# Attention block of a hybrid decoder: last block's transposes, last pair's outputs and two value banks are moved

## The chip, the cores and the metric

One Trainium2 chip, one of its cores. The time is that of one launch on the device in microseconds, the median of several runs. The engines are named as in the profile: PE is TensorE's matmul and PEld its weight load, DVE is VectorE, ACT is ScalarE, POOL is GpSimd, SP is SyncE. They run asynchronously and wait for each other on semaphores. Matmul results land in PSUM banks, from which ACT and DVE read them.

## What is computed

Two pre-norm residual layers over a sequence of 512 tokens with 1024 channels: an S5 state-space layer, then a forgetting attention, each followed by a gated convolutional FFN. The change lies in the attention:

```python
def fox_mixer(h, w_in, b_f, w_out):
    """logit[t,s] = q_t.k_s/sqrt(d) + sum_{s<j<=t} log f_j, causal."""
    proj = h @ w_in
    q = proj[..., :D_MODEL].reshape(Bsz, S, FOX_HEADS, FOX_HEAD_DIM) * (FOX_HEAD_DIM ** -0.5)
    k = proj[..., D_MODEL:2 * D_MODEL].reshape(Bsz, S, FOX_HEADS, FOX_HEAD_DIM)
    v = proj[..., 2 * D_MODEL:3 * D_MODEL].reshape(Bsz, S, FOX_HEADS, FOX_HEAD_DIM)
    f_logit = proj[..., 3 * D_MODEL:]
    log_f = jax.nn.log_sigmoid((f_logit + b_f).astype(f32))
    F = lax.cumsum(log_f, axis=1).transpose(0, 2, 1)
    ...
        s = jnp.einsum('bhqd,bshd->bhqs', q_blk, k).astype(f32)
        s = s + Fq[..., None] - F[:, :, None, :]
        s = jnp.where(causal, s, -jnp.inf)
        p = jax.nn.softmax(s, axis=-1)
        return jnp.einsum('bhqs,bshd->bqhd', p.astype(v.dtype), v)
    ...
    return o @ w_out
```

There are 16 heads of 64 channels, that is 8 pairs of heads, and 4 blocks of 128 queries. All is float32 at the surface.

## The kernel before

Every large product is done in three matmuls: each operand is split into a high part (a rounded copy, made on ACT) and a low part (the rest, made on DVE), and high x high, high x low and low x high are accumulated in one PSUM bank. `put_parts` (L236 and L237) does such a split: one ACT copy, then one DVE subtraction. Weights arrive by DMA as `raw`, are split into `w_hi` and `w_lo`, and are used at L253 (`mms`).

PSUM has eight banks, in two pools of four: `mm` (tile name `mmp`) and `aux`. A new tile of a pool takes the pool's banks in turn and has to wait until the last reader of its bank is done. The program's text is not always the order of issue: the framework arranges the instructions of each engine when the kernel is built, by when it takes their operands to be ready, and on the chip each engine then goes through its own list in order.

The attention runs as follows.

- `fox_values` (L1104) computes the values and the forget gates' logits. `values` (L1125) takes a set of value quarters `q` and token blocks `b`, holds one bank for each (q, b), and loops over the 8 contraction tiles; then it splits each result into `v` and, for quarter 0, adds the bias to the logits (`ft`, L1143). Group 1 is quarters 0 and 1 on blocks 0 and 1, group 2 the same quarters on blocks 2 and 3, groups 3 and 4 are quarters 2 and 3 on all blocks. During group 1 the norm of the second half of the tokens is still being applied on ACT and DVE (L386 to L390). Behind group 2 the log of the forget gates is computed in many small DVE instructions.
- The query and key projections (L1190) are 16 tiles `m` with 8 contraction tiles each. After each contraction tile (three matmuls, one step) `unit` is called, which counts steps and issues whatever is due at that step.
- When the key tile of pair `hp` is done, `attend` (L1199) enters that pair's work into the list of due steps, by `ORDER` (L48), relative to the step count at that moment: `s0` computes the pair's scores (L1229), the masked minimum on DVE (L1241), the exponential on ACT (L1245), the normalization on POOL (L1250); `t0` to `t3` transpose query block 0 to 3 of the probabilities (L1259) and split them from an aux bank into `phi` and `plo`; `o0` and `o1` (`weigh`, L1267) multiply by the values of the pair's first and second head (L1276), copy and add the result into `ot` (L1282, L1283), and after `o1` split it into `v`'s place as the operand of the output product. So the work of a pair lies between the projections of the next one.
- t0 and t1 take one aux bank each, t2 and t3 two each (one for each head), o0 and o1 one each, the scores four (six for the last pair).
- The output product (`fox`, L1153) does the first four output tiles together (`head=4`): one contraction tile is 12 matmuls, and then `unit(3)` is called, which goes through three steps at once. The work of the last pair therefore lies between the contraction tiles of this head; its own result is the last of the eight contraction tiles, tile 7.

Of the kernel before, what the change touches and what calls it, by code (L numbers as in the profile page):

```python
# [8 lines left out]
F32 = mybir.dt.float32  # L9
# [8 lines left out]
P = 128  # L18
D = 1024
KT = D // P  # L20
S = 512
# [23 lines left out]
QK = 6  # L45


ORDER = ((3, "s0"), (8, "t0"), (8, "t1"), (10, "t2"), (12, "t3"), (17, "o0"), (18, "o1"))  # L48


class Trunk:
# [1019 lines left out]
class Kernel(S5):  # L1071
# [32 lines left out]
    def fox_values(self, pool, x):  # L1104

        nc = self.nc

        self.v = pool.tile([P, KT, NB, 2, 2, HD], F32R, name="v")
        ft = pool.tile([P, NB, NH], F32, name="ft")
        bf = self.fox_bf  # L1110
        W = VH * HD
        xhi, xlo = x

        def load(q):

            src = self.io["fox_v"][q - 1] if q else self.io["fox_vf"]
            n, step = (W, 4) if q else (W + NH, 3)
            out = []
            for a in range(0, KT, step):
                j = min(step, KT - a)  # L1120
                hi, lo = self.split(src[:, a:a + j, :], [P, j, n])
                out += [(hi[:, i, :], lo[:, i, :]) for i in range(j)]
            return out

        def values(qs, blocks, w):  # L1125
            todo = [(q, b) for q in qs for b in blocks]
            ps = {k: self.mm.tile([P, S], F32, name="mmp") for k in todo}
            for k in range(KT):
                for q, b in todo:
                    hi, lo = w[q][k]  # L1130
                    n = W if q else W + NH
                    tb = slice(b * P, (b + 1) * P)
                    for i, (xt, wt) in enumerate(((xhi, hi), (xhi, lo), (xlo, hi))):
                        self.last_mm = nc.tensor.matmul(  # L1134
                            ps[q, b][:, :n], xt[:, k, tb], wt, start=(k == 0 and i == 0), stop=(k == KT - 1 and i == 2),
                        )
                self.finish_norm((k + 1) * len(todo))
            for q, b in todo:
                pv = ps[q, b][:, :W].rearrange("p (g r d) -> p g r d", r=2, d=HD)
                hi, lo = (self.v[:, 2 * q:2 * q + 2, b, :, t, :] for t in range(2))  # L1140
                self.put_parts(hi, lo, pv)
                if q == 0:
                    nc.vector.tensor_tensor(ft[:, b, :], ps[q, b][:, W:W + NH], bf, ALU.add)  # L1143

        w = {q: load(q) for q in range(2)}
        values((0, 1), (0, 1), w)
        values((0, 1), (2, 3), w)
        lf = self.log_forget(ft, pool)
        for q in range(2, NV):
            values((q,), range(NB), {q: load(q)})  # L1150
        return lf
# [47 lines left out]
    def attend(self, pool, hp, q, kk, nfd):  # L1199

        nc = self.nc
        nf = pool.tile([P, 2, 9, P], F32, name="nf")
        nc.sync.dma_start(
            nf.rearrange("p r n k -> p r (n k)"), nfd[2 * hp:2 * hp + 2, :][None].to_broadcast([P, 2, 9 * P])
        )
        for d in (slice(2, 7, 4), slice(7, 9)):
            nc.gpsimd.tensor_tensor(
                nf[:, :, d], nf[:, :, d], self.cmask[:, None, None, :].to_broadcast([P, 2, 2, P]), ALU.add
            )
        logit = (slice(7, 8), slice(0, 9, 8), slice(0, 3), slice(3, 7))  # L1210
        rows = [slice(64 * r, 64 * r + 64) for r in range(2)]
        ss = {}

        def weights(_):

            last = hp == KT - 1
            at = [
                [pl.tile([P, S], F32, name=n) for _ in range(2)]
                for pl, n in ((self.aux, "aux"), (self.aux, "aux"), (self.aux, "aux") if last else (self.mm, "mmp"))
            ]  # L1220
            ps = {}
            for b in range(NB):
                W = (b + 1) * P
                N = max(2 * P, W)
                tq = slice(b * P, W)
                ps[b] = [t[:, 2 * P:] if b == 1 else t[:, :N] for t in at[max(b - 1, 0)]]
                for n, (i, j) in enumerate(((0, 0), (0, 1), (1, 0))):
                    for r, a in enumerate(rows):
                        nc.tensor.matmul(  # L1229
                            ps[b][r], q[i][a, tq], kk[j][a, :N], start=(n == 0), stop=(n == 2),  # L1230
                            tile_position=(64 * r, 0), skip_group_check=True,
                        )
            for b in range(NB):
                W = (b + 1) * P

                s = ss[b] = pool.tile([P, 2, W], F32, name=f"s{b}")
                mn = self.small.tile([P, 2], F32, name="mn", bufs=4)
                sm = self.small.tile([P, 2, 2], F32, name="sm", bufs=4)
                blocks = lambda t: t.rearrange("p (n k) -> p n k", k=P)
                for r in range(2):  # L1240
                    nc.vector.tensor_tensor_reduce(  # L1241
                        blocks(s[:, r]), blocks(ps[b][r][:, :W]), nf[:, r, logit[b]], -1.0, -NEG, ALU.add, ALU.min,
                        mn[:, r:r + 1],
                    )
                    nc.scalar.activation(  # L1245
                        s[:, r], s[:, r], AF.Exp, scale=-1.0, bias=mn[:, r:r + 1], accum_out=sm[:, 0, r:r + 1]
                    )
                nc.vector.reciprocal(sm[:, 1], sm[:, 0])
                for r in range(2):
                    nc.gpsimd.tensor_scalar(s[:, r], s[:, r], sm[:, 1, r:r + 1], 1.0, op0=ALU.mult, op1=ALU.mult)  # L1250

        def turn(b):
            sl = slice(b, 4 * b + 1, 3)
            s = ss.pop(b)
            for rs in ((0, 1),) if b < 2 else ((0,), (1,)):
                pt = self.aux.tile([P, len(rs), b + 1, P], F32, name="aux")
                for r in rs:
                    for k in range(b + 1):
                        nc.tensor.transpose(pt[:, r - rs[0], k, :], s[:, r, k * P:(k + 1) * P], self.ident)  # L1259
                h = slice(rs[0], rs[-1] + 1)  # L1260
                self.put_parts(self.phi[:, h, sl, :], self.plo[:, h, sl, :], pt)

        do = {"s": weights, "t": turn, "o": lambda r: self.weigh(hp, r)}
        for n, u in ORDER:
            self.units.setdefault(self.step + n, []).append(lambda u=u: do[u[0]](int(u[1])))

    def weigh(self, hp, r):  # L1267
# [120 lines left out]
```

## Time and profile before

| | |
|---|---|
| median of 3 runs | 1279.46 us (1279.35 to 1281.21) |
| the profiled execution | 1280.95 us, its span 1279.2 us |
| mean granted clock of TensorE | 0.993 |
| values (groups 1 to 4) | 650.3 to 699.7 us |
| query and key projections with pairs 0 to 6 | 700.2 to 839.9 us |
| output product's head with pair 7 | 839.9 to 876.6 us |

The profile is of one execution. Times are counted from the start of its span. A row of the timeline gives the start in microseconds, the duration, the engine, the line, the operation, output <- inputs, shape and count; in brackets stand the idle time of that engine before it and what ended it. "issue" is time for which the profile shows no awaited event. A matmul's end is modelled, and a weight load may run while the previous matmul does, so that a gap between loads shows a standstill more exactly than one between matmuls. A row of the windows gives, for each stretch, its length, the busy time of PE, PEld, DVE, ACT and POOL with their counts, the granted clock of TensorE (1.00 is full speed), the busy share of the DMA engines and their GB/s.

### The profile page before, as it was taken

How to read it: one execution, taken by the hardware profiler on the slowest of the kernel's cores; microseconds unless marked ns; L12 is line 12 of the kernel's file. 1: busy time of each engine (PE TensorE's matmuls, PEld its weight loads, DVE VectorE, ACT ScalarE, POOL GpSimd, SP SyncE). 2: the span in 40 equal slices, each digit the busy share in tenths (PEclk: the TensorE clock that was granted, in tenths of full speed). 3: DMA queues.
4: the chain of work that ended last, by engine and by line, in shares of the span. 5: the costliest groups of instructions: out<-in, count | busy, mean ns of one | idle time of the engine just before them, and what ended most of it. 6: DMA issues, size and time to landing. Idle time of an engine off the chain costs nothing.

```text
span 1279.2 us, 17722 instructions
## 1 busy us (share of the span) xinstructions
PE 1256.0 (98%) x6822; PEld 1010.0 (79%) x6822; DVE 773.4 (60%) x1398; ACT 509.9 (40%) x929; POOL 56.6 (4%) x103
## 2 busy tenths in 40 slices
PE   7999999999999999999999999999999999999997
PEld 2566678897877878788899887878988888888887
DVE  8988877478664546764566576655754433444443
ACT  2544455334333223332333566553543322333331
POOL 0000000000000000000000343330000000000000
PEclk9999899999999999999999999999999999999999
DMA  9677666337654645643404433323132233332221
GB/s 370 226 228 248 205 212 219 99 107 246 209 177 130 219 137 193 214 146 116 152 3 132 157 125 123 105 70 99 55 129 93 68 91 128 99 99 82 68 80 67
DMA packets 73060, 183.13 MB, mean 143 GB/s; under 512 B 23079, under 2 KB 25471, under 8 KB 71951
## 3 DMA queue, kind: packets, MB, share of 16 engines
q1 hardware_dynamic: 72687, 181.46, 43.9%
q8 instruction: 54, 0.88, 0.3%
q10 hardware_dynamic: 288, 0.52, 0.1%
q14 instruction: 31, 0.25, 0.1%
HBM read 175.04 MB, written 6.92 MB: 142 GB/s over the span
## 4 chain that ended last, share of the span: by engine, by line
PE 94%; DVE 3%; ACT 2%; DMA 1%; issue 1%; SPq 0%; DVEq 0%; ACTq 0%
PE mmp L253 71%; PE mmp L972 4%; PE mmp L1134 3%; PE aux L778 2%; PE mmp L1001 2%; PE aux L1276 2%; PE mmp L176 1%; PE aux L1259 1%; PE aux L867 1%; PE aux L859 1%; PE aux L1229 1%; DVE w_lo L237 1%; PE mmp L912 1%; PE aux L817 1%; PE mmp L942 1%
## 5 line engine op out<-in xcount | busy, mean ns | idle before, releaser
L253 PE MATMUL mmp<-a_hi,w_hi 128*128 128x512 f32 (+1 forms) x912 | 347.1, 382 | 1.0 <-ACT nm_t L1059 0.7
L253 PE MATMUL mmp<-a_hi,w_lo 128*128 128x512 f32 (+1 forms) x912 | 345.1, 379 | 0.0
L253 PE MATMUL mmp<-a_lo,w_hi 128*128 128x512 f32 (+1 forms) x912 | 344.9, 379 | 0.0
L236 ACT ACTIVATE w_hi<-raw 128x1024 fp32r<-128x1024 f32 (+3 forms) x197 | 190.1, 968 | 386.9 <-PE mmp L253 351.0
L237 DVE TENSOR_TENSOR w_lo<-raw,w_hi 128x1024 fp32r<-128x1024 f32 (+3 forms) x197 | 218.9, 1113 | 198.9 <-ACT w_hi L236 193.4
L253 PEld LDWEIGHTS mmp<-a_hi,w_hi 128*128 128x128 f32 x912 | 170.9, 188 | 35.8 <-issue 2.5
L253 PEld LDWEIGHTS mmp<-a_hi,w_lo 128*128 128x128 f32 x912 | 171.5, 188 | 32.2
L253 PEld LDWEIGHTS mmp<-a_lo,w_hi 128*128 128x128 f32 x912 | 171.7, 188 | 30.6
L253 PE MATMUL mmp<-ghi,w_hi 128*128 128x512 f32 (+1 forms) x396 | 147.7, 373 | 0.0
L253 PE MATMUL mmp<-glo,w_hi 128*128 128x512 f32 (+1 forms) x396 | 147.1, 371 | 0.0
L253 PE MATMUL mmp<-ghi,w_lo 128*128 128x512 f32 (+1 forms) x396 | 147.0, 371 | 0.0
L319 DVE SCALAR_TENSOR_TENSOR h<-mmp,par,h 128x512 f32<-128x512 f32 (+1 forms) x56 | 37.6, 673 | 97.2 <-PE mmp L253 96.9
L253 PEld LDWEIGHTS mmp<-glo,w_hi 128*128 128x128 f32 x396 | 74.9, 189 | 14.0
L253 PEld LDWEIGHTS mmp<-ghi,w_hi 128*128 128x128 f32 x396 | 74.8, 189 | 14.1
L253 PEld LDWEIGHTS mmp<-ghi,w_lo 128*128 128x128 f32 x396 | 74.8, 189 | 14.1
L204 DVE SCALAR_TENSOR_TENSOR ada_acc<-ada_raw,sc,ada_acc 128x1024 f32<-128x1024 f32 x49 | 62.8, 1281 | 27.7 <-DMA ada_raw<-in_ada_w 27.3
L450 DVE TENSOR_TENSOR conv<-conv,mmp 128x512 f32<-128x512 f32 x44 | 30.0, 686 | 64.2 <-PE mmp L253 61.1
L446 ACT ACTIVATE conv<-conv 128x512 f32<-128x512 f32 x44 | 27.6, 632 | 101.4 <-DVE conv L443 101.4
L443 DVE SCALAR_TENSOR_TENSOR conv<-mmp,conv_wb,conv 128x511 f32<-128x511 f32 (+1 forms) x88 | 65.0, 744 | 2.5 <-ACT conv L441 1.5
L972 PE MATMUL mmp<-a_x,raw 128*128 128x512 f32 x112 | 57.5, 652 | 0.0
L253 PE MATMUL mmp<-v,w_hi 128*128 128x512 f32 (+1 forms) x160 | 43.1, 359 | 2.1 <-ACT v L236 2.1
L1245 ACT ACTIVATE s<-s,mn 128x128 f32<-128x128 f32 (+3 forms) x64 | 35.1, 550 | 10.9 <-DVE mn L1241 10.9
(248 smaller groups left out, 1629.2 us busy)
## 6 DMA issues: line engine op xcount, KB each, us to landing
raw<-in_w_up SPq DMA_DIRECT2D x88, 512.0 KB, 3.5
ada_raw<-in_ada_w SPq DMA_DIRECT2D x56, 512.0 KB, 4.3
raw<-in_ada_w SPq DMA_DIRECT2D x40, 512.0 KB, 6.1
raw<-in_w_down SPq DMA_DIRECT2D x32, 384.0 KB, 3.1
raw<-in_w_down SPq DMA_DIRECT2D x32, 320.0 KB, 2.9
nf<-nfd SPq DMA_DIRECT2D x8, 1152.0 KB, 5.7
raw<-in_fox_qk SPq DMA_DIRECT2D x16, 512.0 KB, 3.7
h<-in_x SPq DMA_DIRECT2D x8, 512.0 KB, 5.6
```

The lines of the kernel that those rows point to most:

```text
L204: nc.vector.scalar_tensor_tensor(acc, w, self.sc[:, k:k + 1], acc, op0=ALU.mult, op1=ALU.add)
L236: nc.scalar.activation(hi, src, AF.Copy)
L237: nc.vector.tensor_tensor(lo, src, hi.bitcast(F32), ALU.subtract)
L253: self.last_mm = self.nc.tensor.matmul(o, wt, xt[:, cols], start=(k == 0 and n == 0), stop=(k == nk - 1 and n == 2),)
L319: self.nc.vector.scalar_tensor_tensor(self.h[:, m, cols], ps, self.par[i][:, 16 + m:17 + m], self.h[:, m, cols], op0=ALU.mult, op1=ALU.add,)
L443: nc.vector.scalar_tensor_tensor(t[:, d:], ps[:, :S - d], cw[:, 2 - d, f:f + 1], t[:, d:], op0=ALU.mult, op1=ALU.add)
L446: nc.scalar.activation(t, t, AF.Silu)
L450: nc.vector.tensor_tensor(t, t, ps, ALU.mult)
L778: nc.tensor.matmul(ps[g2][:, j, cols], x[rows, a + j, r].rearrange("p c j -> p (c j)"), self.rr[rows, planes, q, :], start=(j == 0 and r = ...
L972: nc.tensor.matmul(ps, w[m][:, k, :], x[:, k], start=(k == 0), stop=(k == KT - 1))
L1134: self.last_mm = nc.tensor.matmul(ps[q, b][:, :n], xt[:, k, tb], wt, start=(k == 0 and i == 0), stop=(k == KT - 1 and i == 2),)
L1245: nc.scalar.activation(s[:, r], s[:, r], AF.Exp, scale=-1.0, bias=mn[:, r:r + 1], accum_out=sm[:, 0, r:r + 1])
```

## The change

Three edits. `ORDER` issues t3 (the transposes of the fourth query block) one step later, at 13 instead of 12. The last pair gets an order of its own, `LAST`, in which t3 stays at 12 and o0 and o1 come one step earlier, at 16 and 17. And in group 2 of the values, quarter 0's two tiles take aux banks instead of mm banks.

```diff
-ORDER = ((3, "s0"), (8, "t0"), (8, "t1"), (10, "t2"), (12, "t3"), (17, "o0"), (18, "o1"))
+ORDER = ((3, "s0"), (8, "t0"), (8, "t1"), (10, "t2"), (13, "t3"), (17, "o0"), (18, "o1"))
+
+LAST = ((3, "s0"), (8, "t0"), (8, "t1"), (10, "t2"), (12, "t3"), (16, "o0"), (17, "o1"))
...
-        def values(qs, blocks, w):
+        def values(qs, blocks, w, aux=()):
             todo = [(q, b) for q in qs for b in blocks]
-            ps = {k: self.mm.tile([P, S], F32, name="mmp") for k in todo}
+            ps = {
+                k: self.aux.tile([P, S], F32, name="aux") if k in aux else self.mm.tile([P, S], F32, name="mmp")
+                for k in todo
+            }
...
         values((0, 1), (0, 1), w)
-        values((0, 1), (2, 3), w)
+        values((0, 1), (2, 3), w, ((0, 2), (0, 3)))
...
-        for n, u in ORDER:
+        for n, u in LAST if hp == KT - 1 else ORDER:
```

When the last pair is entered, the step count is 128. The head's calls of `unit(3)` go through 128 to 130 after contraction tile 0, 131 to 133 after tile 1, and so on; 143 to 145 after tile 5, 146 to 148 after tile 6. Before, o0 was due at 145 and o1 at 146; with `LAST` they are due at 144 and 145.

## The prediction

> **What bounds the kernel now.** First the page: the busy shares, then the chain by engine.
>
> ```profile
> PE 1256.0 (98%) x6822; PEld 1010.0 (79%) x6822; DVE 773.4 (60%) x1398; ACT 509.9 (40%) x929; POOL 56.6 (4%) x103
> ...
> PE 94%; DVE 3%; ACT 2%; DMA 1%; issue 1%; SPq 0%; DVEq 0%; ACTq 0%
> ```
>
> TensorE is busy nearly all the time and is nearly the whole chain of work that ended last. The change adds and removes no matmul, so it can only win the places where TensorE stands still or runs slowly, and those are few. Next, the waits of PE, and those of its weight loads (PEld), which see a stall better, because a matmul's modelled end covers part of a gap.
>
> ```profile
> PE mmp L253 <- ACT v L236: 2.1, 1, 2.1
> PE aux L1259 <- DVE plo L237: 1.6, 6, 0.4
> ```
> ```profile
> PEld aux L1259 <- issue: 5.1, 12, 0.8
> ```
>
> The columns are total, times, longest. Two of the three waits that the edits are about stand here: the transposes of a pair's last block (L1259, six pairs, two gaps each), and the output product waiting for the last pair's `v`. The third, the second group of values waiting for its banks, is shown at edit 3.
>
> **Edit 1, t3 from step 12 to 13.** Pair 0 has no gap before t3, pair 4 has; the first fence shows the loads of pair 0, the second those of pair 4.
>
> ```profile
> 723.53 0.19 PEld L253 LDWEIGHTS mmp<-a_hi,w_lo 128*128 128x128 f32 x1
> 723.76 1.03 PEld L1259 LDWEIGHTS aux<-rest,s 128*128 128x128 f32 x8
> 724.75 0.19 PEld L253 LDWEIGHTS mmp<-a_hi,w_hi 128*128 128x128 f32 x1
> ```
> ```profile
> 798.25 0.19 PEld L253 LDWEIGHTS mmp<-a_hi,w_lo 128*128 128x128 f32 x1
> 799.07 0.42 PEld L1259 LDWEIGHTS aux<-rest,s 128*128 128x128 f32 x4 [0.64 <-issue]
> 799.67 0.42 PEld L1259 LDWEIGHTS aux<-rest,s 128*128 128x128 f32 x4 [0.18 <-issue]
> 800.06 0.19 PEld L253 LDWEIGHTS mmp<-a_hi,w_hi 128*128 128x128 f32 x1
> ...
> 803.39 0.19 PEld L1276 LDWEIGHTS aux<-phi,v 128*128 128x128 f32 x1
> ```
>
> From the last projection load before t3 to the first behind it: 724.75 - 723.53 = 1.22 us undisturbed, 800.06 - 798.25 = 1.81 in pair 4. The stall costs 0.59 us, not the 0.82 of its two gaps, since stalled loads then run closer. Five pairs are alike; pair 1 has the longest first gap (0.8 against 0.64), so 0.59 + 0.17 = 0.76. Check: 0.81 + 5 x 0.64 + 6 x 0.18 = 5.1, the row's total. In all 0.76 + 5 x 0.59 = 3.7 us.
>
> What t3 waits for stands on VectorE: `plo` of t0 and t1 frees the two aux banks that t3 takes, and it sits behind the split of the next weights.
>
> ```profile
> 797.29 1.33 DVE L237 TENSOR_TENSOR w_lo<-raw,w_hi 128x1024 fp32r<-128x1024 f32 x1 [0.26 <-ACT w_hi L236]
> 798.55 3.20 DVE L237 TENSOR_TENSOR plo<-aux,phi 128x256 fp32r<-128x256 f32 x6
> ```
>
> That queue hangs on the scores (exponentials, `hi`, `w_hi`, `w_lo`, `plo`), which keep their step. So the banks still come free for loads at 799.07 and 799.67. A projection step is three matmuls of 0.23 us (12 take 2.75 in a row further below): the new t3 arrives at 798.25 + 0.23 + 0.69 = 799.17, its second half 0.5 later at 799.67. Both banks are just free: the stall goes wholly in five pairs, and all but 0.07 us of it in pair 1 (0.76 - 0.69). **Edit 1: -3.6 us**, bounded by 0 (the release moves along) and -3.7. t3 issues eight transposes, two ACT copies and two DVE subtractions, no DMA, and passes neither SP's nor POOL's queue.
>
> What is late next: the pair's outputs (o0, load 803.39), now 4 steps behind t3 instead of 5. The six `plo` end at 798.55 + 3.20 = 801.75, with t3 0.1 later at 801.85; o0 comes at 803.39 - 0.59 = 802.80. About 0.95 us stay over: no wait.
>
> **Edit 2, o1 of the last pair one output tile earlier.** The chain around the end of the output product's head:
>
> ```profile
> 865.04 1.29 PE aux L1276 x8
> 866.33 2.75 PE mmp L253 x12
> 869.09 1.30 PE aux L1276 x8
> 870.38 0.02 issue
> 870.40 0.60 ACT ot L1282
> 871.00 0.02 issue
> 871.03 0.70 DVE ot L1283
> ...
> 872.43 7.59 PE mmp L253 x25
> ```
>
> o0, contraction tile 6 (12 matmuls), o1, then tile 7, which needs `v` of this pair: o1's copy, add and split, 872.43 - 870.39 = 2.04 us in a row with nothing left for TensorE. The edit (o0 17 to 16, o1 18 to 17; a head step advances the count by three, so o0 stays in the same call) puts o1 before tile 6. Then o1 runs 866.33 to 867.63, tile 6 to 870.38, and `v` is ready 2.04 after 867.65, say 869.7 (if ScalarE and VectorE are not held by o0's own `ot`: 0.60 + 0.70 from 866.37, done at 867.7, so no more than 0.1 late). The low part follows one 0.69 us subtraction later, 870.4, about when the second matmul of tile 7 reads it: at most 0.1 us of wait. The inputs are there: t3's `plo` is done at 863.85.
>
> ```profile
> 862.56 1.29 DVE L237 TENSOR_TENSOR plo<-aux,phi 128x512 fp32r<-128x512 f32 x2 [2.61 <-ACT phi L236]
> ```
>
> Behind the gap TensorE is slow. The loads of tile 7 (the first five, and the load after its twelve), then the windows, with the granted clock in the third column from the right:
>
> ```profile
> 872.43 1.10 PEld L253 LDWEIGHTS mmp<-v,w_hi 128*128 128x128 f32 x5 [2.27 <-ACT v L236]
> ...
> 876.61 0.46 PEld L253 LDWEIGHTS mmp<-v,w_hi 128*128 128x128 f32 x2
> ```
> ```profile
> 873.00:874.00 1.00, 1.00 (x4) 0.81 (x3) 0.11 (x1) 0.00 (x0) 0.00 (x0) 0.64 0.08 16
> 874.00:875.00 1.00, 1.00 (x4) 0.75 (x3) 0.28 (x1) 0.71 (x1) 0.00 (x0) 0.50 0.00 0
> ```
>
> The twelve take 876.61 - 872.43 = 4.18 us instead of 2.75: 1.4 us more, at half clock, begun three microseconds after TensorE fell idle. Behind edit 3's stall of about 1 us, around 663.5, the clock stays whole:
>
> ```profile
> 664.00:668.00 4.00, 3.90 (x32) 3.93 (x33) 1.02 (x4) 0.17 (x1) 0.00 (x0) 1.00 0.00 0
> ```
>
> I take it that the dip goes with the gap. The load row's 2.27 us is the gap by loads. **Edit 2: -(2.27 - 0.1 + 1.4) = -3.6 us**, bounded by -2.0 (the clock falls anyway, the wait for the low part stays) and -3.7.
>
> [...]
>
> **Edit 3, two value tiles in aux banks.** The last load of group 1 and the first of group 2, then VectorE's add that frees the first bank and the split on the second:
>
> ```profile
> 662.83 0.19 PEld L1134 LDWEIGHTS mmp<-w_hi,a_lo 128*128 128x128 f32 x1
> 664.07 0.19 PEld L1134 LDWEIGHTS mmp<-w_hi,a_hi 128*128 128x128 f32 x1 [1.05 <-ACT v L236]
> ```
> ```profile
> 663.79 0.17 DVE L1143 TENSOR_TENSOR ft<-mmp,rest 128x16 f32<-128x16 f32 x1
> 663.87 0.41 DVE L237 TENSOR_TENSOR v<-mmp,v 128x256 fp32r<-128x256 f32 x1
> ```
>
> At 0.12 us a load, group 2 could begin at 662.95; it loses 1.12. The tiles (0,2) and (0,3) now take aux banks; those next in turn were last read by the norm's first half, and no aux bank is wanted again before the first pair's scores, behind all four groups. Their six matmuls (0.75 us) run in the gap; (1,2) takes the mm bank that was freed for 664.07, so 0.37 us of wait remain, and (1,3), 0.37 later, finds its bank about in time (its split ends at 664.28, then an add as the first). **Edit 3: -0.75 us**, bounded by -1.1 (the issue order lets (0,2) and (0,3) run ahead) and 0. The third group, too, finds free banks, but that is worth nothing: the fourth waits for VectorE, which works through forget gates and splits from group 2's end without a pause.
>
> ```profile
> 687.93 0.19 PEld L1134 LDWEIGHTS mmp<-w_hi,a_hi 128*128 128x128 f32 x1 [0.34 <-DVE v L237]
> ```
>
> **The sum.** 3.6 + 3.6 + 0.75 = 7.95 us. The profiled execution took 1280.95 us (span 1279.2), so 1273.0 by it; the three runs shown have a median of 1279.46, 1.5 below, and the forecast is 1279.46 - 7.95 = **1271.5 us**, 0.62% faster.
>
> **The rivals.** (a) *The dip stays* (above): 1271.5 + 1.4 = 1272.9. For: its cause isn't seen; against: it is the only dip here. (b) *The wait moves along with t3*: if `plo` of t0 and t1 is issued yet later on VectorE, edit 1 gives nothing, 1275.1. For: pair 0 has another issue order than pairs 1 to 6, so the order isn't fixed by the text alone; against: nothing ahead of those `plo` depends on t3. (c) *The change doesn't do what it says in the tail*: o1 is issued behind tile 6 as before, edit 2 gives nothing, 1275.1. Against: its operands and bank are free by 864. (d) *Slower*: ScalarE's next weight split gets issued ahead of t3's copies.
>
> ```profile
> 799.83 1.20 ACT L236 ACTIVATE phi<-aux 128x512 fp32r<-128x512 f32 x2 [1.08 <-PE aux L1259]
> 802.22 1.06 ACT L236 ACTIVATE w_hi<-raw 128x1024 fp32r<-128x1024 f32 x1 [1.20 <-PE mmp L253]
> ```
>
> That `w_hi` waits for the end of a projection, 9 matmuls behind t3 today, 6 with the change. If it goes first: 801.63 + 1.06 = 802.69, `w_lo` 1.33 more, then a `plo` of 0.65: o0's operand at 804.7 instead of its 802.80, 1.9 us lost in each of six pairs. Edit 1 becomes -3.6 + 11.4, and the total -7.95 + 11.4 = +3.4: 1282.9; if gaps of 1.9 us also bring half clock, up to 6 x 1.4 more, 1291. It decides only if t3's copies come ready after the projection ends; by these rows they lead by more than a microsecond. (e) *No visible change*: two of the three edits fail together, 1277 to 1279.
>
> **How the numbers follow.** Forecast (1270 to 1272.5) 0.62; (a) 0.10; (b) 0.10; (c) 0.05; (e) 0.07; (d) 0.06. A measurement here tells about 0.2% (2.6 us) from no change. Faster by more: 0.62 + 0.10 + 0.10 + 0.05 = 0.87; within: 0.07; slower: 0.06. The range goes from the sum of the upper bounds, 3.7 + 3.7 + 1.1 = 8.5 (1271.0), less 1 us for the spread of runs, to (b) and (c) with half a microsecond: 1270.0 to 1275.6.
>
> **What would show it.** Right: PEld's gaps at L1259 fall from 5.1 us to under 0.5; the pair period shrinks by 0.59 us; o0 and o1 of the last pair stand together, tile 7 follows tile 6 without a wait for `v`, with clock 1.00; group 2 begins within 0.2 us of group 1's end. Wrong: a new wait at L1276 (d), a wait for `plo` as long as before (b), clock 0.50 without a gap (a).

## The result and the profile after

The changed kernel takes 1271.55 us (median of 6 runs, 1271.17 to 1272.8), the kernel before 1279.4 in the same comparison (6 runs, 1278.35 to 1281.21). The ratio is 0.994, its 95% interval 0.9927 to 0.9953: 7.85 us less, where 7.95 were forecast. The profiled execution took 1272.8 us with a span of 1271.0; the span of before was 1279.2. A line of the kernel that stood at L1134 is now L1139; L253, L1229, L1259 and L1276 are now L255, L1234, L1264 and L1281.

First the page of after, busy times and the chain by engine:

```profile
PE 1252.1 (99%) x6822; PEld 1009.2 (79%) x6822; DVE 775.2 (61%) x1398; ACT 509.3 (40%) x929; POOL 57.0 (4%) x103
...
PE 96%; DVE 2%; DMA 1%; ACT 1%; issue 0%; SPq 0%; DVEq 0%; ACTq 0%
```

The same 6822 matmuls fill a larger share of a shorter span. **Edit 1**: the weight loads of t3 in pair 4, the row that had two gaps before.

```profile
796.26 0.19 PEld L255 LDWEIGHTS mmp<-a_hi,w_lo 128*128 128x128 f32 x1
796.49 1.02 PEld L1264 LDWEIGHTS aux<-rest,s 128*128 128x128 f32 x8
797.48 0.19 PEld L255 LDWEIGHTS mmp<-a_hi,w_hi 128*128 128x128 f32 x1
```

The eight loads stand in one piece, and from the load ahead to the load behind it is 1.22 us, where before it was 1.81. In the list of what weight loads wait for, one row is left for L1264, the one for POOL in pair 0 (0.5 us, as before). **Edit 2**: the chain at the end of the output product's head, then the loads around the start of tile 7, then the windows.

```profile
857.92 2.77 PE mmp L255 x12
860.69 2.59 PE aux L1281 x16
863.28 16.82 PE mmp L255 x74
```
```profile
863.00 0.31 PEld L255 LDWEIGHTS mmp<-v,w_hi 128*128 128x128 f32 x2
...
865.64 0.19 PEld L255 LDWEIGHTS mmp<-v,w_hi 128*128 128x128 f32 x1
866.07 0.19 PEld L255 LDWEIGHTS mmp<-v,w_hi 128*128 128x128 f32 x1 [0.24 <-DVE v L239]
...
868.49 0.41 PEld L255 LDWEIGHTS mmp<-v,w_hi 128*128 128x128 f32 x2
```
```profile
864.00:866.00 2.00, 2.00 (x10) 1.50 (x9) 1.30 (x2) 0.63 (x1) 0.00 (x0) 1.00 0.00 0
866.00:868.00 2.00, 2.00 (x10) 1.61 (x9) 1.17 (x3) 1.39 (x2) 0.00 (x0) 1.00 0.04 8
```

o0 and o1 are one piece of 16 matmuls, tiles 6 and 7 run through behind them, and of the wait for `v` 0.24 us are left, for the low part. Tile 7's twelve matmuls take 868.49 - 865.64 = 2.85 us; before they took 4.18, behind a gap of 2.27. The clock is 1.00. **Edit 3**: the last load of group 1, the first of group 2, its first load into an mm bank, and group 4's first.

```profile
663.08 0.19 PEld L1139 LDWEIGHTS mmp<-w_hi,a_lo 128*128 128x128 f32 x1
663.20 0.19 PEld L1139 LDWEIGHTS aux<-w_hi,a_hi 128*128 128x128 f32 x1
...
664.33 0.19 PEld L1139 LDWEIGHTS mmp<-w_hi,a_hi 128*128 128x128 f32 x1
...
687.20 0.19 PEld L1139 LDWEIGHTS mmp<-w_hi,a_hi 128*128 128x128 f32 x1 [0.41 <-DVE v L239]
```

Group 2 follows group 1 by 0.12 us, the ordinary distance. The list of TensorE was arranged anew with the edit: the tiles in aux banks come first and fill the time until 664.33. At group 4 the wait for VectorE is 0.41 us where it was 0.34.

**Where the 8.2 us of the span went.** Three landmarks, each the load that starts a piece of work: group 1 of the values, the scores of pair 0, the scores of the last pair. First before, then after.

```profile
650.22 0.19 PEld L1134 LDWEIGHTS mmp<-w_hi,a_hi 128*128 128x128 f32 x1
...
713.74 0.19 PEld L1229 LDWEIGHTS aux<-hi 64*128 64x128 f32 x2 [0.35 <-issue]
...
848.22 0.19 PEld L1229 LDWEIGHTS aux<-hi 64*128 64x128 f32 x2 [0.36 <-issue]
```
```profile
650.48 0.19 PEld L1139 LDWEIGHTS mmp<-w_hi,a_hi 128*128 128x128 f32 x1
...
713.04 0.19 PEld L1234 LDWEIGHTS aux<-hi 64*128 64x128 f32 x2 [0.35 <-issue]
...
843.86 0.19 PEld L1234 LDWEIGHTS aux<-hi 64*128 64x128 f32 x2 [0.36 <-issue]
```

The fourth landmark is the first load behind tile 7's twelve, 876.61 and 868.49. So: up to group 1, where nothing was changed, +0.26; group 1 to pair 0 (edit 3) 63.52 to 62.56, -0.96; pair 0 to the last pair (edit 1) 134.48 to 130.82, -3.66; the last pair to the end of tile 7 (edit 2) 28.39 to 24.63, -3.76; from there to the end 402.59 to 402.51, -0.08. The sum is -8.2.

### The profile page after: what moved, and what is told of

It reads as the page before. It is cut to its first block, busy times and chain, and to the rows that moved or that the text cites. A ratio compares the mean times of both kernels' runs of the same rounds, so it can differ in the third digit from the quotient of the medians.

```text
span 1271.0 us, 17722 instructions
## 1 busy us (share of the span) xinstructions
PE 1252.1 (99%) x6822; PEld 1009.2 (79%) x6822; DVE 775.2 (61%) x1398; ACT 509.3 (40%) x929; POOL 57.0 (4%) x103
## 4 chain that ended last, share of the span: by engine, by line
PE 96%; DVE 2%; DMA 1%; ACT 1%; issue 0%; SPq 0%; DVEq 0%; ACTq 0%
PE mmp L255 73%; PE mmp L974 4%; PE mmp L1139 2%; PE aux L780 2%; PE mmp L1003 2%; PE aux L1281 2%; PE aux L1264 1%; PE mmp L178 1%; PE aux L869 1%; PE aux L861 1%; PE aux L1234 1%; PE mmp L914 1%; PE aux L819 1%; PE mmp L944 1%; PE aux L212 1%; PE aux L139 1%
## 5 line engine op out<-in xcount | busy, mean ns | idle before, releaser
L255 PE MATMUL mmp<-a_hi,w_hi 128*128 128x512 f32 (+1 forms) x912 | 347.1, 382 | 1.0 <-ACT nm_t L1061 0.7
L255 PE MATMUL mmp<-a_hi,w_lo 128*128 128x512 f32 (+1 forms) x912 | 345.1, 379 | 0.0
L255 PE MATMUL mmp<-a_lo,w_hi 128*128 128x512 f32 (+1 forms) x912 | 344.9, 379 | 0.0
L255 PEld LDWEIGHTS mmp<-a_hi,w_hi 128*128 128x128 f32 x912 | 170.9, 188 | 36.0 <-issue 2.6
L255 PEld LDWEIGHTS mmp<-a_hi,w_lo 128*128 128x128 f32 x912 | 171.5, 188 | 32.1
L255 PEld LDWEIGHTS mmp<-a_lo,w_hi 128*128 128x128 f32 x912 | 171.6, 188 | 30.5
L255 PE MATMUL mmp<-ghi,w_hi 128*128 128x512 f32 (+1 forms) x396 | 147.7, 373 | 0.0
L255 PE MATMUL mmp<-glo,w_hi 128*128 128x512 f32 (+1 forms) x396 | 147.1, 371 | 0.0
L255 PE MATMUL mmp<-ghi,w_lo 128*128 128x512 f32 (+1 forms) x396 | 147.0, 371 | 0.0
L255 PEld LDWEIGHTS mmp<-ghi,w_hi 128*128 128x128 f32 x396 | 74.8, 189 | 14.1
L255 PEld LDWEIGHTS mmp<-glo,w_hi 128*128 128x128 f32 x396 | 74.9, 189 | 14.0
L255 PEld LDWEIGHTS mmp<-ghi,w_lo 128*128 128x128 f32 x396 | 74.8, 189 | 14.1
L255 PE MATMUL mmp<-v,w_hi 128*128 128x512 f32 (+1 forms) x160 | 42.1, 351 | 0.1
```

Of the source, the lines that this page charges most:

```text
L255: self.last_mm = self.nc.tensor.matmul(o, wt, xt[:, cols], start=(k == 0 and n == 0), stop=(k == nk - 1 and n == 2),)
```

## The experiments

All of them compute the whole result. They ran in three groups, each beside runs of before: the edits alone and t3 in mm banks (before: 1280.25 us), then t3 at 14 and 15, after without edit 2 and o1 behind one tile (1278.97), then the other four (1279.89). Single runs of before lie between 1275 and 1284 there, so a stage tells more than a whole run. The three stages are those of the ledger above, each from its own profile; "dip" says whether half clock followed the gap ahead of tile 7, in the last stage (no word: the profile has no gap of 2 us there, and no dip).

| kernel | median, us | ratio, 95% interval | group 1 to pair 0 | pair 0 to last pair | last pair to end of tile 7 |
|---|---|---|---|---|---|
| before | | | 63.52 | 134.48 | 28.39, dip |
| after | 1271.55 | 0.994, 0.9927 to 0.9953 | 62.56 | 130.82 | 24.63 |
| edit 1 alone | 1276.39 | 0.9974, 0.9959 to 0.999 | 63.53 | 130.83 | 28.43, dip |
| edit 2 alone | 1276.97 | 0.9973, 0.9958 to 0.9989 | 63.51 | 134.46 | 24.63 |
| edit 3 alone | 1279.07 | 0.9994, 0.9979 to 1.001 | 62.52 | 134.41 | 28.39, dip |
| t3 in mm banks | 1275.1 | 0.9971, 0.9953 to 0.9988 | 63.52 | 130.97 | 26.87, no dip |
| after, t3 at 14 | 1272.02 | 0.9934, 0.9913 to 0.9956 | 62.49 | 130.76 | 24.60 |
| after, t3 at 15 | 1276.02 | 0.9974, 0.9958 to 0.999 | 62.56 | 134.14 | 24.62 |
| after without edit 2 | 1275.39 | 0.9972, 0.9956 to 0.9987 | 62.53 | 130.86 | 28.45, dip |
| after, o1 behind one tile | 1272.53 | 0.9946, 0.993 to 0.9961 | 62.54 | 130.87 | 24.80 |
| before, again | 1278.93, one run | | 63.58 | 134.51 | 26.83, no dip |
| after without edit 2, again | 1276.79, one run | | 62.52 | 130.99 | 28.12, dip |
| after, t3 at 17 | 1278.1, one run | | 62.53 | 136.61 | 24.60 |
| after, group 4 in aux banks too | 1271.84 | 0.9935, 0.9917 to 0.9953 | 62.05 | 130.87 | 24.63 |

**Each edit alone.**

```diff
-ORDER = ((3, "s0"), (8, "t0"), (8, "t1"), (10, "t2"), (12, "t3"), (17, "o0"), (18, "o1"))
+ORDER = ((3, "s0"), (8, "t0"), (8, "t1"), (10, "t2"), (13, "t3"), (17, "o0"), (18, "o1"))
+LAST = ((3, "s0"), (8, "t0"), (8, "t1"), (10, "t2"), (12, "t3"), (17, "o0"), (18, "o1"))
```

Edit 1:

> The kernel before with edit 1 alone (t3 at step 13 in pairs 0 to 6, the last pair and the values as before). Theory (t3 waited for banks whose release stays where it is): the gaps of PEld at the transposes fall from 5.1 us to under 0.5, the time by 3.6 us, to 1275.8 us. Rival (the release moves along with t3): the gaps stay, 1279.4 us.

```diff
 ORDER = ((3, "s0"), (8, "t0"), (8, "t1"), (10, "t2"), (12, "t3"), (17, "o0"), (18, "o1"))
+LAST = ((3, "s0"), (8, "t0"), (8, "t1"), (10, "t2"), (12, "t3"), (16, "o0"), (17, "o1"))
```

Edit 2:

> The kernel before with edit 2 alone (o0 and o1 of the last pair one output tile earlier). Theory: the gap ahead of tile 7 and the half clock behind it go together, 3.7 us, 1275.7 us with the granted clock 1.00 from there to the end. Rival (the dip of the clock isn't the gap's and stays): 2.3 us, 1277.1 us, with a window of clock 0.5 to 0.64 still there. Rival (o1 is issued behind tile 6 as before): 1279.4 us.

```diff
-        values((0, 1), (2, 3), w)
+        values((0, 1), (2, 3), w, ((0, 2), (0, 3)))
```

Edit 3:

> The kernel before with edit 3 alone (two value tiles of group 2 in aux banks). Theory: the wait of 1.05 us at group 2's first load goes, group 4's wait on VectorE becomes a little longer, 1.0 us gained in all, 1278.4 us. As the prediction had it, with 0.37 us of wait left: 0.75 us, 1278.7 us. Rival (the wait only moves to group 4): 1279.4 us.

Each edit changes its own stage by as much as in after (-3.65, -3.76, -1.00) and the other two by less than 0.1. With edit 2 alone the clock is 1.00 in each of the four windows from 868 to 876 us, around tile 7. The medians agree with that: 3.3 us by the ratio 0.9974 of 1280.25, 3.5 by 0.9973; for edit 3 alone the interval holds no change, as an edit of one microsecond must give here.

**What t3 waits for.**

```diff
-                pt = self.aux.tile([P, len(rs), b + 1, P], F32, name="aux")
+                pl, n = (self.mm, "mmp") if b == 3 and hp < KT - 1 else (self.aux, "aux")
+                pt = pl.tile([P, len(rs), b + 1, P], F32, name=n)
```

> The kernel before, t3 at its step 12, but in pairs 0 to 6 its two tiles are taken from the four mm banks instead of the aux banks. Theory (t3 waits for the aux banks that the low parts of t0 and t1 hold): the gaps at the transposes go without any move, 3.6 us, 1275.8 us. Rival (t3 waits for its probabilities, or for its place in the steps): the gaps stay at 5.1 us, 1279.4 us. If the projections then wait for the banks that t3 holds, new gaps show at their loads.

The loads of t3 in pair 1, which had the longest gap, at its old step 12 but in other banks:

```profile
740.43 0.19 PEld L253 LDWEIGHTS mmp<-a_hi,w_lo 128*128 128x128 f32 x1
740.66 1.02 PEld L1260 LDWEIGHTS mmp<-rest,s 128*128 128x128 f32 x8
741.65 0.19 PEld L253 LDWEIGHTS mmp<-a_hi,w_hi 128*128 128x128 f32 x1
```

Without any move the 1.22 us are back, and the stage falls by 3.5 us (134.48 to 130.97). So it was the banks, not the probabilities and not the step. The 0.15 us that it falls short of edit 1 lie ahead of pair 1.

**How far t3 can go.** In `ORDER` of after:

```diff
-(13, "t3")
+(14, "t3")
```

> The kernel after with t3 two steps later than before (14 instead of 13). Theory: nothing waits for t3 yet (its low parts end about 800.0 us in pair 4, the outputs' first load comes at 800.3), so 1271.5 us, at most 0.5 more. Rival (t3 at 13 uses up all the slack of the outputs): gaps at the outputs of seven pairs, 0.5 to 0.7 us each, about 1276 us.

```diff
-(13, "t3")
+(15, "t3")
```

> The kernel after with t3 at step 15. In the program as built, ScalarE's next weight split then stands ahead of t3's copies in pairs 0 to 6, which is the prediction's slower rival. Theory: the outputs of a pair wait some 1.6 to 1.9 us each in seven pairs, 11 to 13 us, so 1283 to 1285 us, and more if half clock follows those gaps (1.4 us each: up to 1294). Rival (the order on ScalarE doesn't matter, the outputs have enough slack): 1271.5 to 1273 us.

At 14 nothing changes (130.76 us in the stage). At 15 the stage is 3.3 us longer than in after. ScalarE's queue in pair 2, and TensorE's wait:

```profile
760.25 1.06 ACT L238 ACTIVATE w_hi<-raw 128x1024 fp32r<-128x1024 f32 x1 [1.91 <-PE mmp L255]
761.21 1.07 ACT L238 ACTIVATE phi<-aux 128x512 fp32r<-128x512 f32 x2
```
```profile
PEld aux L1281 <- DVE plo L239: 4.6, 7, 1.3
```

The order that the slower rival feared is there: `w_hi` goes ahead of t3's copies, and the outputs wait for `plo`. The wait came out at 4.6 / 7 = 0.66 us for a pair, not 1.6 to 1.9, and the stage lost 3.3 / 7 = 0.47. In pair 2, ScalarE's part of the price did not come: `w_hi` ran from 760.25 to 761.31 beside t3's own transposes (760.28 to 761.31), and t3's copies followed at once; only `w_lo` on VectorE stood ahead of t3's `plo`. And TensorE's list was arranged anew as well: two projection matmuls (0.46 us) now stand between the first matmul of the outputs, which needs only `phi`, and the second, which needs `plo`. I had taken TensorE's list as fixed. The expected 1283 to 1285 us were a miss; measured were 1276.02.

**Does half clock belong to the gap?** Edit 2 taken out of after:

```diff
-LAST = ((3, "s0"), (8, "t0"), (8, "t1"), (10, "t2"), (12, "t3"), (16, "o0"), (17, "o1"))
+LAST = ((3, "s0"), (8, "t0"), (8, "t1"), (10, "t2"), (12, "t3"), (17, "o0"), (18, "o1"))
```

> The kernel after without edit 2 (edits 1 and 3 stay, so the gap ahead of tile 7 stands some 4.6 us earlier in the program's time than in the kernel before). Theory: the gap of 2.3 us is back and half clock follows it, 1275.2 us, a window with clock 0.5 to 0.64 about three microseconds behind the gap's start. Rival (the dip came at a time of its own, not from the gap): the gap without a dip, 1273.8 us.

And o1 behind the first of tile 6's four output tiles (s0 and t3 are counted one step later, so that they keep their place behind a whole contraction tile):

```diff
-                    for m in ms[:head]:
+                    for j, m in enumerate(ms[:head]):
                         self.mms(ps[m][:, c], wk[m], x, k, nk, c)
+                        if step and j == 0:
+                            step(1)
                     self.finish_norm((k + 1) * head)
                     if step:
-                        step(3)
+                        step(2)
...
-LAST = ((3, "s0"), (8, "t0"), (8, "t1"), (10, "t2"), (12, "t3"), (16, "o0"), (17, "o1"))
+LAST = ((4, "s0"), (8, "t0"), (8, "t1"), (10, "t2"), (13, "t3"), (17, "o0"), (18, "o1"))
```

> The kernel after, but o1 of the last pair is issued behind the first of the four output tiles of contraction tile 6, not ahead of all of them. Some 2.06 us of TensorE's work lie then between o1 and tile 7 where 2.75 are, so a gap of about 0.4 to 1.6 us opens at tile 7. Theory (half clock follows only a gap of about 2 us): no dip, 1272 to 1273.1 us. Rival (any gap at this place brings it): 1.4 us more, 1273.4 to 1274.5 us.

The first brought gap and dip back together. The second opened a gap of only 0.43 us by loads, without a dip, and cost 0.17 us in its stage. But the kernel with t3 in mm banks has the old gap of 2.06 us (by matmuls) and no dip behind it, and neither theory allowed for that. Half clock behind tile 7's gap lasts 3.41 us (in before from 873.28 to 876.69), and within one profile the dips start at whole multiples of 3.413 us from each other, those long before the attention too (in before 40.42, 136.00 and 873.28: 28 and 216 times). Three runs were put to that. (The first expectation says that every dip so far lasted 3.41 us; the one at 136.00 in before and the one at 136.30 in after last twice that, 6.83 us.)

> The kernel before, unchanged, profiled once more. The dips of the profiles so far last 3.41 us each and start at whole multiples of 3.413 us from each other within one profile. Theory (the clock is set anew in windows of 3.413 us that run on by themselves; half clock follows a window that holds nearly all of the gap of 2.06 us): counted from the earlier dips of this same profile, half clock starts at the first boundary behind the gap, unless a boundary cuts the gap so that no window holds more than about 1.4 us of it; then there is none, and the time behind the gap is 1.6 us shorter. Rival (the gap starts a delay of its own): half clock starts 2.3 to 2.9 us after the gap's start in any case.

> The kernel after without edit 2, profiled once more, for the same question as the kernel before profiled once more: by the theory half clock behind the gap of 2.06 us starts at a boundary of the 3.413 us windows, or is missing where a boundary cuts the gap near its middle; by the rival it starts 2.3 to 2.9 us after the gap's start.

> The kernel after with t3 at step 17, right ahead of the pair's outputs, so that the outputs wait for t3's split in seven pairs. From the rows of t3 at 15, where the wait came out at 0.25 to 1.3 us, I expect gaps of 1 to 2.5 us, 7 to 15 us in all: 1279 to 1287 us, and 1.6 us more for each gap that brings half clock. Theory of the free-running windows: of these seven gaps those that lie for about 2 us or more within one window bring half clock, the others not, and each dip starts at a boundary. Rival (the length of the gap alone decides): gaps of the same length all bring it or none does.

The kernel before, again: first TensorE's row with the gap in brackets, then the windows.

```profile
872.07 1.42 PE L253 MATMUL mmp<-v,w_hi 128*128 128x512 f32 x5 [2.06 <-ACT v L236]
```
```profile
41.80:42.00 0.20, 0.20 (x2) 0.00 (x0) 0.20 (x1) 0.20 (x1) 0.00 (x0) 0.97 0.00 0
137.40:137.60 0.20, 0.20 (x3) 0.15 (x2) 0.20 (x2) 0.20 (x3) 0.00 (x0) 0.91 0.77 276
868.00:871.40 3.40, 2.00 (x12) 1.59 (x10) 0.69 (x1) 0.60 (x2) 0.00 (x0) 1.00 0.00 0
871.40:874.80 3.40, 2.73 (x12) 2.28 (x13) 1.74 (x3) 1.89 (x3) 0.00 (x0) 1.00 0.02 5
```

A window of 0.2 us with a mean clock of 0.91 is at half clock for 0.09 / 0.5 = 18% of it, its last 0.036 us: that dip starts at 137.564, and the earlier one at 41.988. The distance is 95.576 us, 28 times 3.4134. Counted on from 137.564 by 3.41333 (the distance in before, 737.280 us, by 216), the 215th boundary is at 871.43. It cuts the gap (870.01 to 872.07) into 1.42 and 0.64 us, and there is no dip. Tile 7's twelve matmuls take 2.63 us:

```profile
872.07 0.99 PEld L253 LDWEIGHTS mmp<-v,w_hi 128*128 128x128 f32 x5 [2.27 <-ACT v L236]
...
874.70 0.42 PEld L253 LDWEIGHTS mmp<-v,w_hi 128*128 128x128 f32 x2
```

The kernel after without edit 2, again:

```profile
868.69 1.53 PE L255 MATMUL mmp<-v,w_hi 128*128 128x512 f32 x5 [2.06 <-ACT v L238]
```
```profile
136.00:136.20 0.20, 0.20 (x4) 0.20 (x2) 0.20 (x2) 0.20 (x2) 0.00 (x0) 0.57 1.00 410
866.40:869.80 3.40, 1.34 (x7) 0.95 (x7) 1.38 (x2) 1.22 (x2) 0.00 (x0) 1.00 0.02 5
869.80:870.00 0.20, 0.20 (x2) 0.12 (x1) 0.00 (x0) 0.00 (x0) 0.00 (x0) 0.73 0.00 0
870.00:873.20 3.20, 3.20 (x9) 2.51 (x8) 2.25 (x3) 2.94 (x4) 0.00 (x0) 0.50 0.00 0
```

Here the earlier dip starts at 136.028 and the one in the tail at 869.892; between them are 733.864 us, 215 times 3.4133. The window from 866.48 to 869.89 holds the whole gap (866.63 to 868.69), and half clock follows, 3.26 us after the gap's start, outside the rival's 2.3 to 2.9. (This dip ends behind the last landmark, at 872.58, so 28.12 us in the table hold only a part of it.) The same count fits the first profile of before and the kernel with t3 in mm banks:

```profile
135.80:136.00 0.20, 0.20 (x4) 0.20 (x4) 0.20 (x2) 0.20 (x2) 0.00 (x0) 0.99 0.78 307
873.20:873.30 0.10, 0.10 (x2) 0.06 (x1) 0.00 (x0) 0.00 (x0) 0.00 (x0) 0.88 0.00 0
873.30:876.60 3.30, 3.30 (x9) 2.53 (x8) 1.68 (x3) 2.31 (x3) 0.00 (x0) 0.50 0.02 5
```
```profile
136.20:136.40 0.20, 0.20 (x4) 0.20 (x4) 0.20 (x1) 0.20 (x2) 0.00 (x0) 0.89 0.76 307
863.40:866.80 3.40, 2.02 (x12) 1.60 (x10) 0.69 (x1) 0.59 (x1) 0.00 (x0) 1.00 0.00 0
866.80:870.20 3.40, 2.72 (x12) 2.25 (x13) 1.72 (x3) 1.88 (x3) 0.00 (x0) 1.00 0.02 5
```

Before: 873.276 - 135.996 = 737.280, 216 times 3.41333. With t3 in mm banks the boundary at 866.81 cuts the gap into 1.39 and 0.67: no dip. So in these four profiles one count of 3.413 us that runs on through the gap fits what was measured: the dip starts on it in before and in after without edit 2, again, 2.91 and 3.26 us after the gap's start, and where it cuts the gap there is none. The traces show where the dips start, not what sets the clock. At this place a window in which TensorE was busy for 1.34 of 3.4 us was followed by half clock, one with 2.00 was not.

The third run told nothing of it:

```diff
-(13, "t3")
+(17, "t3")
```

The expected gaps of 1 to 2.5 us did not come, since TensorE's list was again filled with projection matmuls; the longest wait for t3 was 0.87 us, no dip came, and the stage grew by 136.61 - 130.82 = 5.8 us, to 1278.1 in all. Pair 3 of it:

```profile
784.93 0.19 PEld L1281 LDWEIGHTS aux<-phi,v 128*128 128x128 f32 x1 [0.39 <-ACT phi L238]
...
786.80 0.19 PEld L1281 LDWEIGHTS aux<-plo,v 128*128 128x128 f32 x1 [0.87 <-DVE plo L239]
```

**Group 4 in aux banks too.**

```diff
-            values((q,), range(NB), {q: load(q)})
+            values((q,), range(NB), {q: load(q)}, ((3, 0), (3, 1)))
```

> The kernel after, with the first two tiles of the fourth group of values in aux banks too. Theory: group 4's wait for VectorE (0.41 us, the third group's gain given back) goes or shrinks, 0.4 us gained, 1271.1 us, less than these runs can tell from 1271.5. Rival: group 4 waits for the split of its bank's tile anyway, no change in the wait.

```profile
686.18 0.19 PEld L1139 LDWEIGHTS mmp<-w_hi,a_lo 128*128 128x128 f32 x1
686.30 0.19 PEld L1139 LDWEIGHTS aux<-w_hi,a_hi 128*128 128x128 f32 x1
```

The wait is gone and the stage is 0.51 us shorter than in after (62.56 to 62.05). In the time of whole runs that can't be told from after: 0.9935 (0.9917 to 0.9953) against 0.994 (0.9927 to 0.9953). By its stage it is the better version, by half a microsecond.

## Why the prediction was right

**Edit 1 (forecast -3.6, measured -3.66).** Its mechanism held: the banks as the cause (shown by t3 in mm banks), 0.59 us for the loads of a pair instead of the 0.82 of their gaps, and the slack of the outputs: 0.95 us were worked out, t3 one further step of 0.69 us later costs nothing, two steps later it does. From scores to scores the four periods from pair 2 to pair 6 shrank by 0.63 to 0.64 us (18.8 to 18.16) and the last one by 0.46, so the sum agrees better than its parts. Rival (b), that the release moves along, is refuted.

**Edit 2 (forecast -3.6, measured -3.76 between these two profiles).** The gap went and rival (c) with it. The low part's wait was sized at 0.1 and is 0.24 us; the dip was sized at 1.4 and costs 4.18 - 2.63 = 1.55, since the undisturbed twelve matmuls behind a gap take 2.63, not 2.75. These nearly cancel. What was wrong is the sentence "I take it that the dip goes with the gap": of the seven profiles with the gap of 2.06 us five have the dip. In those it starts 2.3 to 2.9 us after the gap's start in four and 3.26 in one, less than 3.41, so that the whole gap lies between two boundaries; in the two without a dip a boundary cuts the gap (1.42 + 0.64 and 1.39 + 0.67 us). And "it is the only dip here", in rival (a), was misread: before has two more long before the attention, at 40.42 and 136.00, with no gap of this size ahead of them (TensorE is busy for 3.13 and 3.32 of the 3.40 us ahead), and one at the kernel's very end, at 1276.05. The gap itself is worth 26.83 - 24.63 = 2.20 us, by the profile of before that has no dip; the 1.55 of the dip came on top in the other. As an estimate from these numbers: if the position of the windows is by chance, the dip comes in (3.413 - 2.06) / 3.413 = 40% of executions when the whole gap has to be inside, and in up to (3.413 - 2.06 + 2 x 0.64) / 3.413 = 77% when just over 1.42 us of it suffice (0.64 may then stick out on either side). That is 0.6 to 1.2 us on average, so by this estimate edit 2 is worth 2.8 to 3.4 us in the mean, not 3.6. The forecast took the profile that happened to show the dip; the difference is less than the spread of the runs. Rival (a), that the dip stays, is refuted by edit 2 alone, whose stage is as short as that of after (24.63 us), and none of the seven profiles without the gap has a dip there (24.60 to 24.80 us).

**Edit 3 (forecast -0.75, measured -0.96 in after and -1.00 alone).** The 0.37 us of wait that the text's order would leave were not there, since the list of TensorE was arranged anew: the upper bound of 1.1 us had named this case. Group 2 itself starts 1.13 us earlier against group 1 (13.85 to 12.72 us), 0.17 more than the stage gained; group 4's longer wait (0.41 instead of 0.34) is 0.07 of that, and the rest was not followed up. With group 4 in aux banks the whole wait goes, 0.51 us of the stage.

**Rival (d), slower.** Its order of ScalarE's list is real, it sets in two steps later than the change goes, and its price was 0.66 us of wait for a pair instead of 1.9: `w_hi` ran beside t3's transposes in the pair shown, and TensorE's list adapts too.

**The sum.** By stages 0.96 + 3.66 + 3.76 = 8.4, less the 0.26 that the stages ahead of group 1 took more, plus 0.08 behind: 8.2 between the two profiles, 7.85 between the medians. With the dip by its mean the sum is 7.4 to 8.0. That 7.95 and 7.85 differ by only 0.1 us is in part luck: edit 3 came out larger than forecast, edit 2 is worth less in the mean, and the interval of the ratio allows 6.0 to 9.3 us.

## What to carry to other kernels

When a transpose or matmul waits for a bank, look for what stands ahead of the bank's release on the reading engine: a move by the length of the stall (here one step of 0.69 us for a stall of 0.59), or two banks of a pool that has them free at that time, removed the wait here (1.22 us from load to load in either), and taking the tile from the other pool shows which of the two it was. A matmul chain that ends a stage and whose result needs a split should be issued one independent tile before the consumer (here 2.75 us of tile 6 over 2.04 us of copy, add and split: of the wait of 2.27 us 0.24 were left). Read a clock dip as a chance, not as a part of the gap: here the gap of 2.06 us had one behind it in five profiles of seven. Look whether the count from earlier dips of the same profile (3.413 us here) puts a boundary into the gap before you count its gain, and compare kernels stage by stage when such dips come and go.

## What the runs showed of the hardware that was not expected

Within one execution the dips of the granted clock start at whole multiples of 3.413 us from each other, over most of a millisecond: 216 of them in before (737.280 us), 215 in after without edit 2, again (733.864 us), right to a few hundredths of a microsecond. The same gap of 2.06 us had half clock behind it in five profiles and not in two; in those two a boundary of that count falls into the gap.

The dips in the first part of the kernel come and go too. The windows of the first 200 us, before, then edit 3 alone:

```profile
0.00:100.00 100.00, 91.65 (x588) 49.18 (x588) 85.21 (x257) 42.41 (x109) 1.31 (x20) 0.98 0.79 274
100.00:200.00 100.00, 99.20 (x781) 69.48 (x780) 76.91 (x114) 48.74 (x128) 0.00 (x0) 0.97 0.70 220
```
```profile
0.00:100.00 100.00, 91.07 (x594) 49.53 (x594) 85.89 (x258) 42.39 (x109) 1.31 (x20) 1.00 0.80 276
100.00:200.00 100.00, 99.20 (x792) 70.73 (x791) 80.15 (x117) 51.73 (x131) 0.00 (x0) 1.00 0.72 228
```

The span of the latter was 1274.0, 5.2 us less than before, while its changed stage gained 1.0; most of the difference is there when group 1 starts, at 646.27 instead of 650.22. Busy time as the profile shows it did not decide alone here. In the first profile of before, the window ahead of the dip at 136.00 is full of matmuls, but of small ones (inputs of 128x64 and 64x80, where the large ones have 128x512). In the second, the window from 24.92 to 28.33 (33 windows ahead of 137.564) holds only 1.48 us of matmuls, since TensorE stands still until 26.82, and no half clock follows. First the window and the dip of the one, then the window of the other and what follows it:

```profile
132.60:136.00 3.40, 3.32 (x32) 3.10 (x32) 3.40 (x9) 1.02 (x4) 0.00 (x0) 1.00 0.93 342
136.00:142.80 6.80, 6.80 (x14) 3.09 (x13) 3.37 (x7) 3.54 (x14) 0.00 (x0) 0.50 0.50 164
```
```profile
24.90:28.30 3.40, 1.48 (x5) 0.67 (x4) 3.30 (x9) 0.18 (x1) 0.00 (x0) 1.00 1.02 411
28.40:31.70 3.30, 3.30 (x17) 0.89 (x20) 3.30 (x7) 0.00 (x0) 0.00 (x0) 1.00 1.03 410
```

So the 1.34 and 2.00 us of the output product's head are no threshold for other matmuls. Which work in a window goes with full clock behind it, and whether the small matmuls are what brings the early dips, was not tried.
